# Neighbourhood attention with tokens in halves of the grid's columns: five transposes per pair of heads, and products with v over 128 and over 32 keys

## The chip, the cores and the metric

One core of one Trainium2 chip. The metric is the device time of one execution in microseconds; a smaller one is better. TensorE (PE in the rows, its weight loads PEld) multiplies and transposes, VectorE (DVE), ScalarE (ACT) and GpSimd (POOL) do the rest, and SyncE (SP) issues the transfers. Each has its own queue and works it off in order.

## The reference

Two layers, each with a gated feed-forward block, a mixer block and a second feed-forward block, with a layer norm behind every block. 256 tokens of 1024 numbers stand on a grid of 4 rows and 64 columns. The mixer projects x once and feeds three mixers: pooling over 2 to 16 neighbouring tokens, a short gated convolution, and neighbourhood attention. Its core:

```python
scores = jnp.einsum('brqhd,brikhd->bhrqik', q, kb).astype(jnp.float32) * (NA_HEAD_DIM ** -0.5)
scores = scores + bias.astype(jnp.float32)
scores = jnp.where(col_valid[:, None, :], scores, NEG_INF)
p = jax.nn.softmax(scores, axis=(-2, -1)).astype(v.dtype)
o = jnp.einsum('bhrqik,brikhd->brqhd', p, vb)
```

With 4 rows, every query sees all rows; in each it sees 16 of the 64 columns, chosen by its own column. There are 8 heads of 64 numbers. All is float32; the big products run as three products of float32r parts (upper by upper, upper by lower, lower by upper).

## The kernel before

**Tiling.** The tokens are two tiles of 128 (t), in the order of the sequence, so each tile has two grid rows. Each block streams its weights: SP loads 512 KB into one of 6 raw buffers (`raw`, L206), ACT casts it to float32r (`whi`, L218), DVE subtracts (`wlo`, L223), and TensorE multiplies (L345 to L347 with x stationary, L358 to L360 with the weights stationary, L370 to L372 for the projection back).

**Order of the work.** All engines take their instructions in the order in which the program is written. A `Pacer` keeps a clock of the work given to TensorE so far: `step(us)` moves it on, and hooks put in with `at(delay, tag, fn)` are written out at the first step behind their due time. So a delay such as A_TR sets after how many projection matmuls a piece stands on TensorE, and in what place on the others; it waits for nothing by itself. The waits come from the data and from the buffers.

**Attention.** The mixer projects v and the pooling input, then q0, k0, q1, k1 (four heads each), gc and h, and then the way back. For each half of the heads (q = 0, 1) there are two pairs of heads (j = 0, 1), and each pair goes through four hooks:

- `scores`: a block b of 128 queries is half of the columns (32) in all 4 rows. Each block and head (e) gets one product with 160 keys (4 rows of KW = 40 columns, L799), in a bank of the pool `acc`. DVE adds bias and mask (L808) and takes the maximum (L810); ACT takes the exponential (L813) into `pz`, a buffer of zeros that has all 64 columns per row.
- `normalise`: DVE multiplies by the inverse sum (L823, L825).
- `transposed`: `pz` has zeros outside of the 40 columns, so 256 keys are transposed per block and head: four transposes per head (L834) into one bank, and one copy by ACT (L839, `PT`).
- `weighted`: products of v with PT over 128 keys twice, 256 queries at once (L848), for both heads into one bank; ACT casts the result for each block (L861, `yT`) and DVE takes the lower part (L862).

The banks for projections, transposes and products come from one pool of four (`bank()`, tag mm); a fifth use waits until an earlier one has been read. The work tiles Sb and PT come from a pool of five. The bias of the second half is added by POOL (L690).

Of the kernel before, what the change touches and what calls it, by code (L numbers as in the profile page):

```python
# [16 lines left out]
P = 128  # L17
SEQ = 256
# [24 lines left out]
PZ = 4  # L43
# [14 lines left out]
A_TR = 2.2  # L58
A_PV = 1.4
# [85 lines left out]
def encoder_kernel(  # L145
# [14 lines left out]
    tp = ctx.enter_context(tc.tile_pool(name="tp", bufs=5))  # L160
    ap_ = ctx.enter_context(tc.tile_pool(name="ap", bufs=6))
# [18 lines left out]
    def mirrored(v):  # L180

        dims = [list(d) for d in v.ap]
        step, n = dims[-1]
        dims[-1] = [-step, n]
        return bass.AP(tensor=v.tensor, offset=v.offset + (n - 1) * step, ap=dims)

# [179 lines left out]
    def r_stat(ps, key, act, t, n, first, last, c=slice(0, 512), again=False):  # L366

        hi, lo = pc.get(key)
        ts = slice(t * P, (t + 1) * P)
        PE.matmul(ps, act[0][:, ts], hi[:, n, c], start=first, stop=False, skip_group_check=again)  # L370
        PE.matmul(ps, act[1][:, ts], hi[:, n, c], start=False, stop=False, skip_group_check=again)  # L371
        PE.matmul(ps, act[0][:, ts], lo[:, n, c], start=False, stop=last, skip_group_check=again)  # L372
# [13 lines left out]
    def ln_rest(t, stats, store):  # L386
# [9 lines left out]
        for c in hs:  # L396
            DVE.scalar_tensor_tensor(xt[:, c], xt[:, c], rs[:, 0:1], b[:, c], ALU.mult, ALU.add)
            if store:
                SP.dma_start(out[0, t * P : (t + 1) * P, c], xt[:, c])
# [68 lines left out]
    def ffn(key, xT, next_gb, stop, store=False):  # L468
# [69 lines left out]
        def act(k):  # L538
            f = k[-1]
            return [hts[f // 2][:, i, f % 2, :] for i in range(2)]  # L540
# [62 lines left out]
    def setup():  # L603
# [61 lines left out]

        pz = []
        for i in range(PZ):
            z = cp.tile([P, 2, ROWS, GRID], F32, tag=f"pz{i}", name=f"pz{i}")
            POOL.memset(z, 0.0)
            pz.append(z)  # L670
        consts.update(pz=pz, npz=0)
# [26 lines left out]
    def mixers(l, xT, next_gb, stop):  # L698
# [7 lines left out]
        v = hp.tile([P, NT, 512], F32, tag="h", name=nm("v"))  # L706
        U = ap_.tile([P, 2, SEQ + 2 * PADL], F32, tag="a", name=nm("U"))
# [5 lines left out]
        def pool_means():  # L713
# [15 lines left out]
            def product():  # L729
# [4 lines left out]
                for j in range(2):  # L734
                    c = 12 + l * 2 + j
                    ACT.activation(ya[:, j, :], ps[:, j, :], AF.Copy, scale=cw[:, c : c + 1])
# [6 lines left out]
        for t in range(NT):  # L743
# [3 lines left out]
            ACT.copy(v[:, t, :], pv)  # L747
            pc.step(6 * MM512)
# [5 lines left out]
            def spread(t=t, un=un):  # L754
# [3 lines left out]
                ACT.copy(U[:, :, PADL + t * P : PADL + (t + 1) * P], tr[:, 0:2, :])  # L758
# [12 lines left out]
        def conv_mixer(z):  # L771
# [6 lines left out]
            DVE.tensor_tensor(s, s, GB, ALU.mult)  # L778
            new_y(1)
            ACT.copy(ys[1][:, 0], s)  # L780
            DVE.tensor_tensor(ys[1][:, 1], s, f32(ys[1][:, 0]), ALU.subtract)

        def attention(j, qT, kT, q):

            st = {}
            new = [consts["pz"][(consts["npz"] + e) % PZ] for e in range(2)]
            consts["npz"] += 2
            tag = f"a{q}"

            def inner(z, b):  # L790
                return z[:, b, :, b * KOFF : b * KOFF + KW]

            def scores():
# [9 lines left out]
                st["sm"] = []  # L803
                for e in range(2):
# [7 lines left out]
                    for b in range(2):  # L812
                        ACT.activation(  # L813
                            inner(new[e], b), Sb[:, b, :].rearrange("p (i k) -> p i k", k=KW),
                            AF.Exp, bias=mx[:, b : b + 1], accum_out=sm[:, b : b + 1],
                        )
                    st["sm"].append(sm)
                pc.at(A_NORM, tag, normalise)

            def normalise():  # L820
                for e in range(2):
                    sm = st["sm"][e]
                    DVE.reciprocal(sm, sm)  # L823
                    for b in range(2):
                        DVE.tensor_scalar(inner(new[e], b), inner(new[e], b), sm[:, b : b + 1], None, ALU.mult)  # L825
                pc.at(A_TR, tag, transposed)

            def transposed():
                st["PT"] = []
                for e in range(2):  # L830
                    tr = bank().rearrange("p (a b) -> p a b", a=2)
                    for kc in range(2):
                        for b in range(2):
                            PE.transpose(  # L834
                                tr[:, kc, b * P : (b + 1) * P],
                                new[e][:, b, 2 * kc : 2 * kc + 2, :].rearrange("p r c -> p (r c)"), ident,
                            )
                    t_ = tp.tile([P, 2, SEQ], F32, tag="t", name=nm("PT"))
                    ACT.copy(t_, tr)  # L839
                    st["PT"].append(t_)  # L840
                pc.at(A_PV, tag, weighted)

            def weighted():
                po = bank()[:, 0:SEQ].rearrange("p (b r c) -> p b r c", b=2, r=ROWS)
                for kc in range(2):
                    for e in range(2):
                        c0 = (4 * q + 2 * j + e) * HD
                        PE.matmul(  # L848
                            po[e * 64 : e * 64 + 64], v[:, kc, c0 : c0 + HD], st["PT"][e][:, kc, :],
                            start=(kc == 0), stop=(kc == 1),  # L850
                        )
# [3 lines left out]
                for b in range(2):  # L855
                    src = mirrored(po[:, b])
                    dst = [
                        y[:, i, j, :].rearrange("p (r c) -> p r c", c=GRID)[:, :, b * QB : (b + 1) * QB]
                        for i in range(2)
                    ]  # L860
# [5 lines left out]
        def qk(q):  # L866
            pq = proj(f"q{q}")
            qT = hp.tile([P, 2, 2, P], F32, tag="qk", bufs=4, name=nm("qT"))
            for j in range(2):
                for b in range(2):  # L870
                    src = mirrored(pq[:, j, :].rearrange("p (r c) -> p r c", c=GRID)[:, :, b * QB : (b + 1) * QB])
# [87 lines left out]
```

## Time and profile before

| | us |
|---|---|
| median of 3 runs | 949.89 (949.8 to 949.92) |
| the profiled execution | 950.0 |
| its span, first to last instruction | 948.2 |
| TensorE busy | 938.1 (99%) |
| DVE, ACT, POOL busy | 577.5, 447.0, 60.9 |
| transposes L834, busy | 8.9 (64 of them) |
| products L848, busy | 7.8 (64 records of 32 products) |
| scores L799, busy | 5.4 (64 records of 32 products) |

A matmul of float32 operands shows as two records. Records overlap, because the array is pipelined: what a matmul costs is the distance from its start to the next one's start, not its duration. "x16" merges neighbours of one kind. The chain of work lists, in order of time, what ended last; a wait is put down to the engine and line that released it.

### The profile page before, as it was taken

Reading aid. Unit: us, or ns where it says so; the run is one execution under the profiler, and the core shown is the slowest. Engines: PE = TensorE matmul, PEld = TensorE weight load, DVE = VectorE, ACT = ScalarE, POOL = GpSimd, SP = SyncE. Lnnn points to the kernel's source line nnn. Section 1 sums busy time; section 2 is a strip of 40 time slices with the busy share of each in tenths; the row PEclk is TensorE's granted clock in tenths of the full one; section 3 lists DMA queues with packets and bytes.
Section 4 is the critical chain, followed back from the end, with each engine's and each line's share of the span. In section 5 each row is a group of like instructions: output and inputs, shape, how many; then the busy total and the mean of one; then the engine's idle time right before and its main releaser. Section 6 shows DMA issues by size and latency. Waiting matters only on the chain.

```text
span 948.2 us, 12782 instructions
## 1 busy us (share of the span) xinstructions
PE 938.1 (99%) x4819; PEld 793.6 (84%) x4819; DVE 577.5 (61%) x723; ACT 447.0 (47%) x622; POOL 60.9 (6%) x106
## 2 busy tenths in 40 slices
PE   9999999999999999999999999999999999999996
PEld 6888888989988888888888888888898888888895
DVE  5854454686777654555675555557777875554535
ACT  6644444346735544443444444444565554444420
POOL 4000100005100000000000001000060000000000
PEclk9999999999999999999999999999999999999999
DMA  9877486447444866655458657654645457656401
GB/s 324 304 256 226 107 297 194 133 139 239 153 137 156 270 233 185 196 182 163 144 172 264 233 157 224 212 173 143 201 151 174 156 188 249 217 189 194 161 1 45
DMA packets 96590, 178.81 MB, mean 189 GB/s; under 512 B 14784, under 2 KB 35856, under 8 KB 96528
## 3 DMA queue, kind: packets, MB, share of 16 engines
q1 hardware_dynamic: 96240, 177.60, 58.4%
q8 instruction: 38, 0.62, 0.3%
q10 hardware_dynamic: 288, 0.39, 0.1%
q14 instruction: 24, 0.20, 0.1%
HBM read 176.84 MB, written 1.13 MB: 188 GB/s over the span
## 4 chain that ended last, share of the span: by engine, by line
PE 99%; DVE 1%; ACT 0%; issue 0%; DVEq 0%
PE mm L347 17%; PE mm L345 17%; PE mm L346 17%; PE acc L370 10%; PE acc L371 10%; PE acc L372 10%; PE mm L358 4%; PE mm L360 4%; PE mm L359 4%; PE mm L477 2%; PE mm L323 1%; PE mm L834 1%; PE mm L848 1%; PE acc L799 1%; PE acc L309 0%; PE mm L757 0%
## 5 line engine op out<-in xcount | busy, mean ns | idle before, releaser
L223 DVE TENSOR_TENSOR wlo<-raw,whi 128x1024 fp32r<-128x1024 f32 (+1 forms) x322 | 389.8, 1234 | 209.8 <-ACT whi L218 209.5
L218 ACT CAST whi<-raw 128x1024 fp32r<-128x1024 f32 (+1 forms) x322 | 332.5, 1044 | 319.5 <-PE mm L346 150.6
L345 PE MATMUL mm<-whi,xhi 128*128 128x512 f32 x704 | 275.8, 392 | 0.3 <-ACT whi L218 0.3
L347 PE MATMUL mm<-wlo,xhi 128*128 128x512 f32 x704 | 274.4, 390 | 0.2 <-DVE wlo L223 0.2
L346 PE MATMUL mm<-whi,xlo 128*128 128x512 f32 x704 | 274.0, 389 | 0.0
L347 PEld LDWEIGHTS mm<-wlo,xhi 128*128 128x128 f32 x704 | 132.1, 188 | 28.8 <-DVE wlo L223 1.0
L345 PEld LDWEIGHTS mm<-whi,xhi 128*128 128x128 f32 x704 | 132.3, 188 | 28.4 <-ACT whi L218 1.1
L346 PEld LDWEIGHTS mm<-whi,xlo 128*128 128x128 f32 x704 | 132.3, 188 | 26.9
L370 PE MATMUL acc<-whi,hT 128*128 128x512 f32 (+1 forms) x352 | 138.4, 393 | 0.0
L371 PE MATMUL acc<-whi,hT 128*128 128x512 f32 (+1 forms) x352 | 136.5, 388 | 0.0
L372 PE MATMUL acc<-wlo,hT 128*128 128x512 f32 (+1 forms) x352 | 136.5, 388 | 0.0
L358 PE MATMUL mm<-xhi,whi 128*128 128x256 f32 x320 | 92.0, 287 | 0.0
L360 PE MATMUL mm<-xhi,wlo 128*128 128x256 f32 x320 | 90.5, 283 | 0.0
L359 PE MATMUL mm<-xlo,whi 128*128 128x256 f32 x320 | 90.5, 283 | 0.0
L372 PEld LDWEIGHTS acc<-wlo,hT 128*128 128x128 f32 x352 | 66.1, 188 | 13.6
L482 DVE TENSOR_TENSOR hT<-mm,hT 128x256 fp32r<-128x256 f32 x80 | 32.4, 423 | 73.1 <-ACT hT L481 73.1
L370 PEld LDWEIGHTS acc<-whi,hT 128*128 128x128 f32 x352 | 66.2, 188 | 12.7
L371 PEld LDWEIGHTS acc<-whi,hT 128*128 128x128 f32 x352 | 66.2, 188 | 12.6
L358 PEld LDWEIGHTS mm<-xhi,whi 128*128 128x128 f32 x320 | 61.3, 192 | 1.7 <-issue 1.5
L359 PEld LDWEIGHTS mm<-xlo,whi 128*128 128x128 f32 x320 | 61.3, 192 | 0.3
L360 PEld LDWEIGHTS mm<-xhi,wlo 128*128 128x128 f32 x320 | 61.3, 192 | 0.0
L393 POOL TENSOR_TENSOR rs<-rs,half_t 128x1 f32<-128x1 f32 x12 | 11.7, 979 | 637.5 <-DVE rs L392 637.5
(110 smaller groups left out, 584.2 us busy)
## 6 DMA issues: line engine op xcount, KB each, us to landing
raw<-in_ffn_w_up_dram SPq DMA_DIRECT2D x88, 512.0 KB, 4.6
raw<-in_ffn_w_down_dram SPq DMA_DIRECT2D x88, 512.0 KB, 4.4
raw<-in_ffn_w_gate_dram SPq DMA_DIRECT2D x87, 512.0 KB, 4.6
raw<-in_w_in_dram SPq DMA_DIRECT2D x40, 512.0 KB, 4.1
raw<-in_w_out_dram SPq DMA_DIRECT2D x16, 512.0 KB, 4.9
lng<-in_ln_g_dram SPq DMA_DIRECT2D x6, 512.0 KB, 5.4
lnb<-in_ln_b_dram SPq DMA_DIRECT2D x6, 512.0 KB, 6.5
rbias<-tab SPq DMA_DIRECT2D x16, 96.0 KB, 4.3
```

What stands on the lines that cost most here:

```text
L218: ACT.copy(u, r)
L223: DVE.tensor_tensor(d, r, f32(u), ALU.subtract)
L345: PE.matmul(ps, xT[0][:, kc, ts], hi[:, j, :], start=(kc == 0), stop=False)
L346: PE.matmul(ps, xT[1][:, kc, ts], hi[:, j, :], start=False, stop=False)
L347: PE.matmul(ps, xT[0][:, kc, ts], lo[:, j, :], start=False, stop=(kc == KC - 1))
L358: PE.matmul(o, hi[:, j, c], xT[0][:, kc, :], start=(kc == 0), stop=False)
L359: PE.matmul(o, hi[:, j, c], xT[1][:, kc, :], start=False, stop=False)
L360: PE.matmul(o, lo[:, j, c], xT[0][:, kc, :], start=False, stop=(kc == KC - 1))
L370: PE.matmul(ps, act[0][:, ts], hi[:, n, c], start=first, stop=False, skip_group_check=again)
L371: PE.matmul(ps, act[1][:, ts], hi[:, n, c], start=False, stop=False, skip_group_check=again)
L372: PE.matmul(ps, act[0][:, ts], lo[:, n, c], start=False, stop=last, skip_group_check=again)
L482: DVE.tensor_tensor(h[:, 1, :, ts], src, f32(h[:, 0, :, ts]), ALU.subtract)
```

## The change

A tile of tokens is now one half of the grid's columns in all 4 rows, instead of two whole rows. x is loaded and the result stored in that order (4 pieces of 32 tokens), and what needs the order of the sequence (pooling, convolution, k) is put back by access patterns. With that, v's tile b holds the 128 keys that lie in the columns of block b itself. A block sees 40 columns: 32 of its own, and 8 of the other half, that is 32 keys more. So the probabilities are written as `own` (128 per block and head) and `other` (32 per block and head); four transposes take own, and one takes other for both blocks and both heads at once. The products run over 128 keys (L878) and over 32 keys (L880), the latter in four groups of rows of the array. The 32 keys of v have to stand in the partitions of their group: v is stored to memory and read back in four pieces (`vr`). The exponential stays in place in Sb; the zeroed buffers are gone.

```diff
-PZ = 4
+PZ = 2
-A_TR = 2.2
-A_PV = 1.4
+A_TR = 3.2
+A_PV = 1.6
...
-        queue.dma_start(xs[t][:, c], x[0, t * P : (t + 1) * P, c])
+        src = x[0, :, c].rearrange("(r b q) d -> b r q d", b=NT, q=QB)[t]
+        queue.dma_start(xs[t][:, c], src)
...
+        vr = cp.tile([P, 512], F32, tag="vr", name=nm("vr"))
+        def other_keys():
+            at = tc.dram_tile([P, NT, 512], F32, name=f"v{l}")
+            SP.dma_start(at, v)
+            for b in range(2):
+                c0 = 0 if b == 0 else 2 * QB - KW
+                src = at[:, 1 - b].rearrange("(r c) d -> r c d", c=QB)[:, c0 : c0 + KW - QB]
+                for e in range(2):
+                    SP.dma_start(vr[(2 * b + e) * QB : (2 * b + e + 1) * QB, :], src)
...
             ACT.copy(v[:, t, :], pv)
+            if t == 1:
+                other_keys()
...
             def normalise():
+                own = pzp.tile([P, 2, 2, ROWS, QB], F32, tag="own", name=nm("pz"))
+                other = pzp.tile([P, 2, 2, ROWS, others], F32, tag="other", name=nm("pz"))
...
-                        DVE.tensor_scalar(inner(new[e], b), inner(new[e], b), sm[:, b : b + 1], None, ALU.mult)
+                        for dst, keys in zip((own, other), parts[b]):
+                            DVE.tensor_scalar(
+                                dst[:, b, e], st["S"][e][:, b, :, keys], sm[:, b : b + 1], None, ALU.mult
+                            )
...
             def transposed():
+                own, other = st["pz"]
+                tr = bank().rearrange("p (e b n) -> p e b n", e=2, b=2)
                 for e in range(2):
+                    for b in range(2):
+                        PE.transpose(tr[:, e, b, :], own[:, b, e].rearrange("p r k -> p (r k)"), ident)
+                main = tp.tile([P, 2, 2, P], F32, tag="t", name=nm("PT"))
+                ACT.copy(main, tr)
+                tr = bank()[:, 0:P]
+                PE.transpose(tr, other.rearrange("p b e r k -> p (b e r k)"), ident)
+                other = tp.tile([P, P], F32, tag="t", name=nm("PR"))
+                ACT.copy(other, tr)
...
             def weighted():
-                po = bank()[:, 0:SEQ].rearrange("p (b r c) -> p b r c", b=2, r=ROWS)
+                po = [bank()[:, 0:P] for _ in range(2)]
+                main, other = st["PT"]
+                for long in (True, False):
+                    for b in range(2):
+                        for e in range(2):
+                            c = slice((4 * q + 2 * j + e) * HD, (4 * q + 2 * j + e + 1) * HD)
+                            g = slice((2 * b + e) * QB, (2 * b + e + 1) * QB)
+                            o = po[b][e * 64 : e * 64 + 64]
+                            if long:
+                                PE.matmul(o, v[:, b, c], main[:, e, b, :], start=True, stop=False)
+                            else:
+                                PE.matmul(
+                                    o, vr[g, c], other[g, :], start=False, stop=True, tile_position=(g.start, e * 64)
+                                )
...
-            ACT.copy(kT, pk)
+            for j in range(2):
+                ACT.copy(in_tiles(kT[:, j, :]), tiled(pk[:, j, :]))
```

**Where the pieces stand on TensorE, first half of the heads.** Before, the transposes of both pairs of heads (pz0 to pz3, a bank per head) stand in the projection of k1 (mm_414):

```order
L834 MATMUL mm_416_2300<-ident_101,pz0_733 128x128 [waits DVE_49,PE_49,Pool_49]
L834 MATMUL mm_416_2300<-ident_101,pz0_733 128x128 [waits DVE_49]
L834 MATMUL mm_416_2300<-ident_101,pz0_733 128x128 x2
L834 MATMUL mm_418_2307<-ident_101,pz1_735 128x128 [waits DVE_49,PE_49,Pool_49]
L834 MATMUL mm_418_2307<-ident_101,pz1_735 128x128 [waits DVE_49]
L834 MATMUL mm_418_2307<-ident_101,pz1_735 128x128 x2
L834 MATMUL mm_420_2314<-ident_101,pz2_737 128x128 [waits PE_49,DVE_49,Activation_49,Pool_49]
L834 MATMUL mm_420_2314<-ident_101,pz2_737 128x128 [waits DVE_49]
```

Now they are ten, again in the projection of k1 (mm_419), twelve matmuls later:

```order
L857 MATMUL mm_421_2327<-ident_104,pz_412_2257 128x128 [waits DVE_49,PE_49]
L857 MATMUL mm_421_2327<-ident_104,pz_412_2257 128x128 [waits DVE_49] x3
L861 MATMUL mm_423_2334<-ident_104,pz_413_2258 128x128 [waits DVE_49,PE_49]
L857 MATMUL mm_425_2338<-ident_104,pz_414_2269 128x128 [waits DVE_49,PE_49,Activation_49]
L857 MATMUL mm_425_2338<-ident_104,pz_414_2269 128x128 [waits DVE_49] x3
L861 MATMUL mm_427_2345<-ident_104,pz_415_2270 128x128 [waits DVE_49,Activation_49]
```

The last one's wait for ACT is for the copy of mm_421, whose bank it takes.

**The products of the first half.** Before, they stand between two projections, each pair of heads with one bank:

```order
L848 MATMUL mm_428_2360<-PT_417_2305,v_325_1810 64x256 [waits Activation_49]
L848 MATMUL mm_428_2360<-PT_419_2312,v_325_1810 64x256
L848 MATMUL mm_428_2360<-PT_417_2305,v_325_1810 64x256
L848 MATMUL mm_428_2360<-PT_419_2312,v_325_1810 64x256
L848 MATMUL mm_430_2370<-PT_421_2319,v_325_1810 64x256 [waits Activation_49]
L848 MATMUL mm_430_2370<-PT_423_2326,v_325_1810 64x256 [waits Activation_49]
```

Now they stand inside the next projection (gc, mm_436), between the scores of the second half's first pair of heads (acc_437, acc_438) and those of its second pair. PT is the transposed `own`, PR the transposed `other`:

```order
L816 MATMUL acc_438_2390<-kT_431_2364,qT_411_2252 128x160
L878 MATMUL mm_445_2409<-PT_422_2332,v_325_1805 64x128 [waits PE_49]
L878 MATMUL mm_445_2409<-PT_422_2332,v_325_1805 64x128
L878 MATMUL mm_446_2410<-PT_422_2332,v_325_1805 64x128 x2
L880 MATMUL mm_445_2409<-PR_424_2336,vr_326_1806 64x128 [waits DMAHW6_49]
L880 MATMUL mm_445_2409<-PR_424_2336,vr_326_1806 64x128 [waits DMAHW7_49]
L880 MATMUL mm_446_2410<-PR_424_2336,vr_326_1806 64x128 [waits DMAHW0_49]
L880 MATMUL mm_446_2410<-PR_424_2336,vr_326_1806 64x128 [waits DMAHW1_49]
L878 MATMUL mm_448_2424<-PT_426_2343,v_325_1805 64x128 [waits PE_49,Activation_49]
L878 MATMUL mm_448_2424<-PT_426_2343,v_325_1805 64x128
L878 MATMUL mm_449_2425<-PT_426_2343,v_325_1805 64x128 [waits DVE_49]
L878 MATMUL mm_449_2425<-PT_426_2343,v_325_1805 64x128
```

The wait of mm_449 for DVE is for the subtraction that reads mm_445 (L891). In the second half of the heads the products stand inside the first matmuls of the way back, and the fourth output's wait for DVE there is for the reading of the projection h (L925).

**The same place on ACT.** Before, the four casts of the products (yT, L861) stand ahead of the exponentials of the second half (L813):

```order
L876 COPY kT_427_2358<-mm_414_2272 128x512 [waits PE_49]
L861 CAST yT_429_2365<-mm_428_2360 128x4x32 [waits PE_49]
L861 CAST yT_429_2365<-mm_428_2360 128x4x32 [waits DVE_49]
L861 CAST yT_429_2365<-mm_430_2370 128x4x32 [waits PE_49]
L861 CAST yT_429_2365<-mm_430_2370 128x4x32 [waits DVE_49]
L218 CAST whi_432_2382<-raw_383_2105 128x1024 [waits DMAHW4_49]
L813 ACTIVATE pz0_733,sm_439_2408<-Sb_437_2404,mx_438_2406 128x4x40 [waits DVE_49]
```

Now four exponentials stand ahead of them:

```order
L906 COPY kT_431_2364<-mm_419_2287 128x2x4x32
L228 CAST whi_434_2373<-raw_384_2107 128x1024 [waits DMAHW1_49]
L830 ACTIVATE Sb_439_2395,sm_441_2399<-Sb_439_2395,mx_440_2397 128x160 [waits DVE_49,Activation_49]
L830 ACTIVATE Sb_439_2395,sm_441_2399<-Sb_439_2395,mx_440_2397 128x160
L830 ACTIVATE Sb_442_2402,sm_444_2406<-Sb_442_2402,mx_443_2404 128x160 [waits DVE_49,PE_49,Activation_49]
L830 ACTIVATE Sb_442_2402,sm_444_2406<-Sb_442_2402,mx_443_2404 128x160
L890 CAST yT_447_2419<-mm_445_2409 128x128 [waits PE_49]
L890 CAST yT_447_2419<-mm_446_2410 128x128 [waits PE_49]
```

On SP, the store of v and the four readings of vr stand ahead of the last load of the projection weights (the second half of h). The second layer has the same order throughout.

More of the change, by code (lines that the diff above doesn't have):

```diff
@@ L368, in r_stat @@
         hi, lo = pc.get(key)
[L369 to L372, printed above, removed]
+        PE.matmul(ps, act[0][t], hi[:, n, c], start=first, stop=False, skip_group_check=again)
+        PE.matmul(ps, act[1][t], hi[:, n, c], start=False, stop=False, skip_group_check=again)
+        PE.matmul(ps, act[0][t], lo[:, n, c], start=False, stop=last, skip_group_check=again)
     gbs = []
@@ L539, in act @@
             f = k[-1]
-            return [hts[f // 2][:, i, f % 2, :] for i in range(2)]
+            return [[hts[f // 2][:, i, f % 2, t * P : (t + 1) * P] for t in range(NT)] for i in range(2)]
         def bias_ahead():
@@ L757, in spread @@
                     PE.transpose(tr[:, j, :], un[:, j * P : (j + 1) * P], ident)
-                ACT.copy(U[:, :, PADL + t * P : PADL + (t + 1) * P], tr[:, 0:2, :])
+                dst = U[:, :, PADL : PADL + SEQ].rearrange("p j (r b c) -> p j b r c", b=NT, c=QB)[:, :, t]
+                ACT.copy(dst, tr[:, 0:2, :].rearrange("p j (r c) -> p j r c", c=QB))
                 DVE.tensor_copy(GB[:, :, t * P : (t + 1) * P], tr[:, 2:4, :])
@@ L777, in conv_mixer @@
                     DVE.scalar_tensor_tensor(s[:, j, :], z[:, j, k : k + SEQ], tap[k], s[:, j, :], ALU.mult, ALU.add)
-            DVE.tensor_tensor(s, s, GB, ALU.mult)
+            yb = ap_.tile([P, 2, SEQ], F32, tag="a", name=nm("yb"))
+            for j in range(2):
+                DVE.tensor_tensor(tiled(yb[:, j, :]), in_tiles(s[:, j, :]), tiled(GB[:, j, :]), ALU.mult)
             new_y(1)
-            ACT.copy(ys[1][:, 0], s)
-            DVE.tensor_tensor(ys[1][:, 1], s, f32(ys[1][:, 0]), ALU.subtract)
+            ACT.copy(ys[1][:, 0], yb)
+            DVE.tensor_tensor(ys[1][:, 1], yb, f32(ys[1][:, 0]), ALU.subtract)
         def attention(j, qT, kT, q):
             st = {}
-            new = [consts["pz"][(consts["npz"] + e) % PZ] for e in range(2)]
-            consts["npz"] += 2
             tag = f"a{q}"
-            def inner(z, b):
-                return z[:, b, :, b * KOFF : b * KOFF + KW]
+            others = KW - QB
+            parts = [(slice(b * others, b * others + QB), slice((1 - b) * QB, (1 - b) * QB + others)) for b in range(2)]
             def scores():
@@ L830, in transposed @@
+                tr = bank().rearrange("p (e b n) -> p e b n", e=2, b=2)
                 for e in range(2):
[L831 to L837, printed above, removed]
@@ L852, in weighted @@
+                po = [p_.rearrange("p (r c) -> p r c", r=ROWS) for p_ in po]
                 if ys[2 + q] is None:
@@ L855, in weighted @@
                 for b in range(2):
[L856 to L860, printed above, removed]
+                    src = mirrored(po[b])
+                    dst = [tiled(y[:, i, j, :])[:, b] for i in range(2)]
                     ACT.copy(dst[0], src)
@@ L893, in mixers @@
         POOL.memset(z[:, :, SEQ + 1 :], 0.0)
-        DVE.tensor_tensor(z[:, :, 1 : SEQ + 1], p_, gc, ALU.mult)
+        for j in range(2):
+            DVE.tensor_tensor(in_tiles(z[:, j, 1 : SEQ + 1]), tiled(p_[:, j, :]), tiled(gc[:, j, :]), ALU.mult)
         conv_mixer(z)
```

40 lines of the change are left out of this document (16 added, 24 removed).

## The prediction

> **What bounds the kernel now.** I read the engines' busy shares first, then the chain of work that ended last, then TensorE's waits. The quoted rows are in that order.
>
> ```profile
> PE 938.1 (99%) x4819; PEld 793.6 (84%) x4819; DVE 577.5 (61%) x723; ACT 447.0 (47%) x622; POOL 60.9 (6%) x106
> ...
> PE 99%; DVE 1%; ACT 0%; issue 0%; DVEq 0%
> ...
> PE acc L309 <- DVE zeros L304: 1.5, 1, 1.5
> PE mm L345 <- ACT whi L218: 0.3, 1, 0.3
> PE mm L347 <- DVE wlo L223: 0.2, 1, 0.2
> ```
>
> TensorE is the chain, and it waits 2.0 us in all, at the start of the program. So time moves in two ways only: by what TensorE's own instructions take, and by any new wait on TensorE. Work on ACT, DVE or a queue counts only where TensorE comes to wait for it. The attention's pieces in the chain, in order of time (start, us, what), are these; of the second layer, its transposes:
>
> ```profile
> 240.47 2.36 PE mm L834 x16
> 245.69 1.88 PE mm L848 x16
> 249.19 1.29 PE acc L799 x16
> ...
> 258.71 1.77 PE mm L834 x16
> 263.35 1.88 PE mm L848 x16
> ...
> 706.46 2.37 PE mm L834 x16
> ...
> 724.72 1.77 PE mm L834 x16
> ```
>
> L834 are transposes, L848 the products with v, L799 the scores. One half of the heads (I call them q0 and q1) has 16 transposes, 16 product instructions and 16 score instructions. In q0 the transposes take 2.36 us, in q1 1.77 (0.11 each for 128 columns); q0's are longer because each new group waits for the normalising on DVE.
>
> **Price of a product and of a change of shape.** TensorE's rows around the products and the scores of q0 and q1 (start, us, operation):
>
> ```profile
> 245.29 0.28 PE L359 MATMUL mm<-xlo,whi 128*128 128x256 f32 x1
> 245.41 0.28 PE L360 MATMUL mm<-xhi,wlo 128*128 128x256 f32 x1
> 245.62 1.95 PE L848 MATMUL mm<-PT,v 128*64 128x256 f32 x16
> 247.50 0.39 PE L358 MATMUL mm<-xhi,whi 128*128 128x256 f32 x1
> 247.72 0.28 PE L359 MATMUL mm<-xlo,whi 128*128 128x256 f32 x1
> ...
> 246.32 0.39 PE L848 MATMUL mm<-PT,v 128*64 128x256 f32 x2
> 246.53 0.39 PE L848 MATMUL mm<-PT,v 128*64 128x256 f32 x2
> 246.75 0.39 PE L848 MATMUL mm<-PT,v 128*64 128x256 f32 x2
> ...
> 248.91 0.28 PE L360 MATMUL mm<-xhi,wlo 128*128 128x256 f32 x1
> 249.12 1.36 PE L799 MATMUL acc<-kT,qT 64*128 64x160 f32 x16
> 250.41 0.39 PE L358 MATMUL mm<-xhi,whi 128*128 128x256 f32 x1
> 250.63 0.28 PE L359 MATMUL mm<-xlo,whi 128*128 128x256 f32 x1
> ```
>
> Products already run two at a time (x2): a pair of 256 columns starts every 0.215 us. By columns that is 0.135 for a pair of 160 and 0.108 for 128, near the 0.11 of a 128-column transpose. A block of another tile shape pays at its edges. Into the products the step is 0.21 us (245.41 to 245.62) where 0.12 is usual: 0.09. The block lasts 1.88 us for eight pairs, 1.72: 0.16 more. Behind it the next step is 0.22 instead of 0.12: 0.10. Together 0.35 for two changes of shape. The scores give 0.09, 0.21 (1.29 less eight times 0.135) and 0.10, so 0.40. I take 0.18 per change.
>
> **Transposes.** Ten stand where sixteen stood, 1.10 us at 0.11. The tenth waits: the projection in progress holds one of the four banks, the first three results take the others, so the fourth result needs the first copied out. By the first two of these rows,
>
> ```profile
> L834 PE MATMUL mm<-ident,pz 128*128 128x128 f32 x64 | 8.9, 281 | 0.0
> ...
> L839 ACT COPY PT<-mm 128x512 f32<-128x512 f32 x16 | 8.8, 593 | 2.8 <-PE mm L834 2.4
> ...
> 240.46 0.52 DVE L825 TENSOR_SCALAR pz<-pz,sm 128x160 f32<-128x160 f32 x2
> ```
>
> the fourth transpose starts at 0.33 and takes 0.28, the copy 0.59, and some 0.1 goes to the two handovers (estimate), so the tenth starts at 1.31 and the block ends at 1.42. Against 2.36 and 1.77 that saves 0.94 in q0 and 0.35 in q1, **1.29 per layer**. Without the bank wait it would be 1.93; with q0's normalising still late, about 0.9. I take 1.29: the transposes now stand twelve matmuls later (1.4 us) behind a normalising of 16 shorter instructions instead of 8, which by the third row (0.52 for two of 160 columns) ends some 0.5 us later (estimate).
>
> **Products, apart from waits.** Per half: before, eight pairs of 0.215, 1.72 us. After, 128 columns over 128 keys: eight pairs of 0.108, 0.86; and 128 columns over 32 keys, 16 instructions in four groups of rows and two of columns. The trace shows two tiles side by side, in column groups (L848) and in row groups (L799); four at once it does not show. If four run at once, these are 0.43, if two, 0.86. So the columns save 0.43 or nothing. But shapes now change three times more per half (128 keys, 32, 128, 32 where one shape stood): 3 x 0.18 = 0.54. Net **+0.11** per half by four at once, +0.54 by two. I take four, since both kinds of grouping are seen at work. [...]
>
> **The new wait.** In q0, the changed program runs scores of the first pair of heads, both pairs' products, then scores of the second pair. Each pair's output now takes two banks. Of the four, the projection (mm_436) holds one, mm_445, mm_446 and mm_448 the rest; mm_449 must wait until mm_445 has been read by ACT (L890) and DVE (L891). On ACT that cast stands behind four exponentials of the scores just made. Their chain, from rows of q1 before, and the reading of a product from q0:
>
> ```profile
> 250.04 0.49 DVE L808 TENSOR_TENSOR Sb<-acc,bias 128x320 f32<-128x320 f32 x1
> 250.56 0.49 DVE L810 TENSOR_REDUCE mx<-Sb 128x2 f32<-128x320 f32 x1
> ...
> 251.09 0.43 ACT L813 ACTIVATE pz<-Sb,mx 128x160 f32<-128x160 f32 x1 [1.64 <-DVE mx L810]
> ...
> 252.43 0.41 ACT L813 ACTIVATE pz<-Sb,mx 128x160 f32<-128x160 f32 x1
> ...
> 252.92 0.43 ACT L813 ACTIVATE pz<-Sb,mx 128x160 f32<-128x160 f32 x1
> ...
> 246.75 0.27 ACT L861 CAST yT<-mm 128x128 fp32r<-128x128 f32 x1 [0.44 <-PE mm L848]
> ...
> 247.05 0.29 DVE L862 TENSOR_TENSOR yT<-mm,yT 128x128 fp32r<-128x128 f32 x1 [2.55 <-ACT yT L861]
> ```
>
> From the scores' start (249.12) to the first sum is 0.92; from there to ACT's first slot behind four exponentials 2.88 (252.92); from the cast to the subtraction 0.30, the subtraction 0.29, the handover 0.08 (estimate). So mm_449 may start **4.47 us** after the scores did. TensorE arrives there after four score pairs 0.54, three changes of shape 0.54, four pairs over 128 keys 0.43, the 32-key rounds 0.22, and mm_448's two pairs 0.22: **1.95**. It stands 2.5 us, and behind the waiting row the second scores and the rest of the projection stand too. Bounds: 2.3 with 32-key products two at a time, 3.1 with free changes of shape. In q1 the fourth bank is the projection that DVE reads at once (L925), so no such wait.
>
> **Costed at nothing.** The store of v and its four read-backs enter SP's queue ahead of the last projection load:
>
> ```profile
> 213.01 0.59 ACT L747 COPY v<-mm 128x512 f32<-128x512 f32 x1 [0.49 <-PE mm L347]
> ...
> 223.07 1.05 ACT L218 CAST whi<-raw 128x1024 fp32r<-128x1024 f32 x1 [2.38 <-PE mm L359]
> ...
> raw<-in_w_in_dram SPq DMA_DIRECT2D x40, 512.0 KB, 4.1
> ```
>
> v is ready at 213.6; a store of 512 KB by the last row takes 4.1, four issues 1.7, so that load goes out near 219.5 instead of 213.8 and lands at 223.6. Its cast, by its place in the program, is the one at 223.07: about half a microsecond late on ACT, while TensorE reads those weights after 257. Weight loads behind it are back in step by 223. vr itself lands near 222 and is read near 247. Without this cover, up to 6 us per layer. The strided x and output transfers keep their sizes; kT in two copies, the longer normalising and the shorter PT copies lie beside TensorE's projections.
>
> **Sum.** Per layer: -1.29 + 2 x 0.11 + 2.5 = +1.43; two layers +2.9. The profiled execution took 950.0 us around its span of 948.2, 0.1 above the median of 949.89. So 952.9 by it, **952.8 us** by the median: slower by 0.3%.
>
> **Rivals.**
> *No wait at mm_449* (faster). Place: that row. It decides if mm_445 is free within 1.95 us of the scores' start; then the rest counts alone, 2 x (-1.29 + 0.22): 947.7. For it: before, the cast followed the products by 0.1 (246.75 within the block), so ACT can be prompt. Against it: the four exponentials need these very scores. 6%.
> *The gains eat the wait* (no change). Shape changes between 128 and 32 rows are free and the tenth transpose waits for no bank: -1.93 - 2 x 0.43 + 3.1 = +0.3 per layer, 950.5. Against it: the edges of both blocks above. 12%.
> *Dearer pieces* (slower still). 32-key products go two at a time and each extra change costs 0.36: +1.08 per half; TensorE then arrives 0.75 later and waits 1.75: -1.29 + 2.16 + 1.75 = +2.6 per layer, 955.1. 10%.
> *The array slows after the pause.* The row of q0's products and q1's scores (TensorE, its weights, DVE, ACT, POOL, granted clock, DMA) has the clock at 1.00, without a pause to test it:
>
> ```profile
> 243.00:252.00 9.00, 9.00 (x80) 7.75 (x79) 5.63 (x12) 5.04 (x12) 0.00 (x0) 1.00 0.44 132
> ```
>
> If the clock fell to half for as long as the pause, +1.25 per layer more, 955.3. 5%. [...]
> *My forecast*: 67%.
>
> **How the numbers follow.** The forecast with its own bounds runs from 951.8 to 954.2 (waits of 2.3 to 2.7, halves of 0.0 to 0.5). To hold 8 in 10, I reach halfway to the no-change rival and to the two slower ones: 951.1 to 955.2. A measurement of this kernel tells about 0.2%, 1.9 us, from no change. Faster by more: 6%. Within: 13%, the no-change rival and a sliver of the forecast. Slower: 81%.
>
> **What would show it.** Right: a TensorE wait of 2.2 to 2.8 us per layer just ahead of the third group of 128-key products in q0, released by DVE's subtraction (L891), none in q1; transposes of about 1.4 us in both halves; q1's product block at 2.1 to 2.3 us. Wrong: no such idle, the wait at another row (vr's landing, the normalising), a 32-key block near 0.43 us per pair of heads, or SP's queue holding back weights that TensorE then waits for.

## The result, and the profile after

The changed kernel takes **974.17 us** (median of 5 runs, 972.06 to 975.51) against 949.89 (949.80 to 949.95): 24.3 us more, a ratio of 1.0251 with a 95% interval of 1.0239 to 1.0263. The forecast was 952.8, with a range of 951.1 to 955.2. The profiled execution took 974.46 us around a span of 972.7, against 948.2 before.

Busy time by engine, the chain of work that ended last, and TensorE's waits (us in total, times, longest) in the changed kernel:

```profile
PE 943.9 (97%) x4859; PEld 796.9 (82%) x4859; DVE 580.6 (60%) x759; ACT 443.9 (46%) x626; POOL 52.7 (5%) x102
...
PE 92%; DVE 3%; DMA 2%; issue 1%; ACT 1%; SPq 0%; DVEq 0%; ACTq 0%
...
PE acc L334 <- DMA x<-in_x_dram: 7.3, 3, 3.4
PE mm L878 <- DVE yT L891: 4.5, 2, 2.3
PE acc L320 <- DVE zeros L315: 1.5, 1, 1.5
PE mm L356 <- ACT whi L228: 0.9, 1, 0.9
```

The second wait is the one forecast, at its row, with its releaser: 2.3 us in each layer. The first was not forecast at all. It belongs to the start of the program, where x is transposed for the first time.

To find where 24.5 us of span went, I put the same projection and feed-forward matmuls of the two traces side by side and took the difference of their start times. It stays constant for hundreds of microseconds and steps in four places only. Here it is for all the kernels below (us; the tail is the rest of the difference of the spans). Each trace is of one execution, and that need not be the median one: the one of `after_rows_io` is the slowest of its four, those of the last three `rows2` kernels are the fastest of theirs.

```
                  span    start   layer 0  layer 1   tail
before            948.2
after             972.7  +10.4    +4.0     +5.3     +4.8
before_block_io   964.0  +10.1     0.0      0.0     +5.7
after_plain_io    956.6   -0.1    +4.4     +5.2     -1.2
after_rows_io     963.7   +5.2    +5.7     +5.1     -0.5
after_filled      972.3  +11.0    +4.3     +4.0     +4.8
rows2             960.2   +4.8    +4.9     +2.4     -0.1
rows2_fill10      956.1   +2.9    +2.7     +2.4     -0.1
rows2_pv          953.1   +5.3    -0.2     -0.1      0.0
rows2_pv_pool     950.7   +4.1    -0.9     -0.9     +0.2
repaired          949.4   +2.9    -0.9     -0.9     +0.1
repaired_wait     958.6   +2.9    +3.2     +4.4      0.0
repaired_fill     954.4   +2.9    +1.6     +1.6      0.0
best              947.1   +0.7    -0.9     -0.9     -0.1
```

So 15.2 us of the loss lie at the two ends of the program, outside the attention, and 9.3 in its two layers, where the forecast had 2.9.

**The start.** The share of the 16 DMA engines that is busy (tenths) and GB/s in the first 30 us, in 40 slices; the kernel before, then the change:

```profile
DMA  0039899999999999999997999999999889598998
GB/s 0 0 87 290 265 385 363 328 363 350 352 382 393 385 410 391 393 393 391 385 385 257 126 319 374 330 369 341 371 385 421 352 254 377 199 202 317 311 333 314
```

```profile
DMA  0009426999625899978998997999932222669999
GB/s 0 0 4 90 100 81 191 307 330 385 188 78 130 218 325 371 363 169 191 325 205 167 347 216 147 319 232 298 360 112 98 98 98 98 117 197 382 314 352 396
```

Look at the run of 98s, from 22.5 to 25.5 us: a quarter of the 392 or so that the kernel before reaches, with two tenths of the engines busy. Four of sixteen are working, and four is the number of blocks of 32 rows in the new source of an x load. The trace's completion events of single transfers say the same:

```
transfer                 before                      after
x, tile 0, columns 0:2   16, 2.86 to 3.45            1 at 2.10, then 4, 6.44 to 6.57
x, tile 1, columns 4:8   16, 8.26 to 10.18           1 at 6.77, then 4, 20.35 to 21.40
raw weights behind them  16, 9.67 to 11.51           12, 11.84 to 12.22, and 4, 21.79 to 22.48
```

The weights use all sixteen engines, and a quarter of each load stands in line behind x on the four. Of the 10.4 us at the start, 8.1 is more waiting on TensorE (10.1 against 2.0 in the first 40 us); the rest was not taken apart, but the granted clock was at 0.50 from 7.95 to 11.36 and from 21.62 to 25.01, where the kernel before has it at 1.00. The output's stores are confined in the same way: the first has one event at 956.21 and then 4, from 960.68 to 961.44; before, a store's 16 stand from 945.31 to 945.47. DMA share and rate in 40 slices from 963.0 to the span's end with the change, and from 943.4 to the end before:

```profile
DMA  1100024206001231222222222222222211100000
GB/s 68 51 17 0 0 51 43 9 0 26 0 9 60 60 68 60 85 102 94 102 102 102 102 102 102 102 102 102 102 102 102 102 77 60 43 9 0 0 0 0
```

```profile
DMA  0000000497998989899110000000000000000000
GB/s 0 0 0 0 0 0 0 171 461 307 444 358 341 427 341 427 341 341 342 51 68 0 0 17 0 0 0 0 0 0 0 0 0 0 0 0 0 0 0 0
```

The trace of the kernel before has the same pattern in two small loads. `rows<-in_pool_scale_dram`, with 4 rows outermost, has one event at 68.21 and then 4, from 69.02 to 69.06; `rows<-in_conv_w_dram`, with 12 rows, has one at 67.84 and then 12, from 68.63 to 68.87. What the early event is was not shown.

**The layers.** TensorE's rows of q0 in the first layer: transposes, first scores, products, and the projection behind them (start, us, operation):

```profile
252.22 0.62 PE L857 MATMUL mm<-ident,pz 128*128 128x128 f32 x4
252.76 0.30 PE L861 MATMUL mm<-ident,pz 128*128 128x128 f32 x1
253.15 0.58 PE L857 MATMUL mm<-ident,pz 128*128 128x128 f32 x2
253.94 0.67 PE L857 MATMUL mm<-ident,pz 128*128 128x128 f32 x2 [0.21 <-DVE pz L847]
254.52 0.30 PE L861 MATMUL mm<-ident,pz 128*128 128x128 f32 x1
254.58 0.36 PE L369 MATMUL mm<-xhi,whi 128*128 128x256 f32 x1
...
257.63 0.81 PE L816 MATMUL acc<-kT,qT 64*128 64x160 f32 x8
258.37 0.66 PE L878 MATMUL mm<-PT,v 128*64 128x128 f32 x8
258.96 0.45 PE L880 MATMUL mm<-PR,vr 32*64 32x128 f32 x8
259.33 0.44 PE L878 MATMUL mm<-PT,v 128*64 128x128 f32 x4
262.04 0.44 PE L878 MATMUL mm<-PT,v 128*64 128x128 f32 x4 [2.26 <-DVE yT L891]
262.41 0.45 PE L880 MATMUL mm<-PR,vr 32*64 32x128 f32 x8
...
264.20 0.41 PE L370 MATMUL mm<-xlo,whi 128*128 128x256 f32 x1
264.42 0.41 PE L371 MATMUL mm<-xhi,wlo 128*128 128x256 f32 x1
```

Three things are to be seen. The wait of 2.26 us stands before the third group of 128-key products. Behind it a projection matmul starts every 0.21 us where 0.12 was usual. And q0's transposes run from 252.22 to 254.58, 2.36 us, no shorter than the 2.28 between the same two starts before, because DVE normalises late:

```profile
240.30 2.52 PE L834 MATMUL mm<-ident,pz 128*128 128x128 f32 x16
242.58 0.36 PE L358 MATMUL mm<-xhi,whi 128*128 128x256 f32 x1
```

The granted clock (the third figure from the right) in the stretches with the pause and behind it, both layers:

```profile
257.50:263.00 5.50, 3.24 (x44) 2.02 (x44) 2.63 (x7) 2.69 (x12) 0.00 (x0) 1.00 0.76 270
263.00:268.00 5.00, 5.00 (x29) 4.53 (x28) 3.44 (x7) 2.42 (x11) 0.00 (x0) 0.66 0.06 5
727.50:733.00 5.50, 3.24 (x42) 1.99 (x40) 2.62 (x7) 2.58 (x11) 0.00 (x0) 0.87 0.72 270
733.00:739.00 6.00, 6.00 (x35) 5.15 (x28) 3.48 (x7) 2.29 (x10) 0.00 (x0) 0.55 0.03 2
```

### The profile page after: what moved, and what is told of

Read it like the earlier page. It is cut to its first block, busy times and chain, and to the rows that moved or that the text cites. A ratio compares the mean times of both kernels' runs of the same rounds, so it can differ in the third digit from the quotient of the medians.

```text
span 972.7 us, 12901 instructions
## 1 busy us (share of the span) xinstructions
PE 943.9 (97%) x4859; PEld 796.9 (82%) x4859; DVE 580.6 (60%) x759; ACT 443.9 (46%) x626; POOL 52.7 (5%) x102
## 4 chain that ended last, share of the span: by engine, by line
PE 92%; DVE 3%; DMA 2%; issue 1%; ACT 1%; SPq 0%; DVEq 0%; ACTq 0%
PE mm L356 16%; PE mm L358 16%; PE mm L357 16%; PE acc L380 10%; PE acc L381 10%; PE acc L382 10%; PE mm L369 3%; PE mm L371 3%; PE mm L370 3%; PE mm L487 2%; DMA x<-in_x_dram 2%; DVE wlo L233 1%; PE mm L334 1%; DVE pz L847 1%; DMA raw<-in_w_in_dram 1%
## 5 line engine op out<-in xcount | busy, mean ns | idle before, releaser
L491 ACT CAST hT<-mm 128x256 fp32r<-128x256 f32 x80 | 28.2, 374 | 43.8 <-PE mm L487 23.2
## 6 DMA issues: line engine op xcount, KB each, us to landing
raw<-in_ffn_w_up_dram SPq DMA_DIRECT2D x88, 512.0 KB
raw<-in_ffn_w_down_dram SPq DMA_DIRECT2D x88, 512.0 KB
raw<-in_ffn_w_gate_dram SPq DMA_DIRECT2D x87, 512.0 KB
raw<-in_w_in_dram SPq DMA_DIRECT2D x40, 512.0 KB
raw<-in_w_out_dram SPq DMA_DIRECT2D x16, 512.0 KB
lng<-in_ln_g_dram SPq DMA_DIRECT2D x6, 512.0 KB
lnb<-in_ln_b_dram SPq DMA_DIRECT2D x6, 512.0 KB
```

## The experiments

The theory after the two traces has four causes: x and output transfers on four engines (A); the wait at mm_449, as forecast; the array slowed by that pause (C); DVE late because SP's queue stood still. The rivals are named with each run. Of each edit only the telling lines are shown; ... stands for the others. Each kernel was timed beside the kernel before (949.86 to 949.95 in all groups).

**The transfers, undone and alone.** `after_plain_io` changes the load and the store back:

```diff
-        src = x[0, :, c].rearrange("(r b q) d -> b r q d", b=NT, q=QB)[t]
-        queue.dma_start(xs[t][:, c], src)
+        queue.dma_start(xs[t][:, c], x[0, t * P : (t + 1) * P, c])
...
-                SP.dma_start(out[0, :, c].rearrange("(r b q) d -> b r q d", b=NT, q=QB)[t], xt[:, c])
+                SP.dma_start(out[0, t * P : (t + 1) * P, c], xt[:, c])
```

> The changed kernel, only x loads and output stores as before (128 whole rows per transfer); tokens then stand in another order, so the output is another one, while every instruction on the engines stays. Theory A (an x transfer in four blocks of 32 rows is served by 4 of the 16 DMA engines, so the first loads and the last stores are late): the start gives back 10.4 us and the tail 4.9, so 959 us (958 to 961). Theory B (the late start is the changed setup or the queue's order, the tail something else): the time stays within 2 us of 974.

957.29 us (955.12 to 958.34), 1.0074 of before (1.0059 to 1.0089), 0.7 below the range. Theory A: start and tail are back, the layers keep their loss. The tail is even 1.2 shorter than before: the last stores landed that much sooner behind the same instructions.

`before_block_io` is the same edit the other way round, in the kernel before.

> The kernel before with only the x loads and output stores of the change; token order differs, so the output is another one, the instructions stay. Theory A: 949.9 + 10.4 + 4.9 = 965 us (963 to 967), each x load finished by 4 engines. Theory B: 950 to 952.

967.63 us (965.78 to 968.26), 1.0183 (1.0167 to 1.0198), 0.6 above the range. The two views alone, with no attention changed, cost 15.8 us of span in the fastest of the four, which is the one traced. That is most of the whole loss.

**Rows in one transfer.** `after_rows_io`:

```diff
-        queue.dma_start(xs[t][:, c], src)
+        for r in range(ROWS):
+            r0 = (r * NT + t) * QB
+            queue.dma_start(xs[t][r * QB : (r + 1) * QB, c], x[0, r0 : r0 + QB, c])
```

and likewise for the store, two rows of the grid by SP and two by ACT. The columns of x behind the first two blocks of 128 now come in one go per tile (four transfers), tile 1's issued by ACT.

> The changed kernel, each x load and output store as four transfers of 32 whole rows, half of them issued by ACT. Theory A, if 32 rows spread over all 16 engines: 959 us, plus up to 1.5 for the extra issues at the end (0.35 each). If such a transfer still reaches only 4 engines, or under theory B: 972 to 976.

961.54 us (960.53 to 965.47), 1.0129 (1.0107 to 1.0152), 1.0 above what theory A gave. Every piece now has 16 completion events, and the tail is back to within 0.5 us. The start is still 5.2 late: sixteen transfers instead of six, and SP takes from 3.61 to 9.32 for the issues of the last four, where an issue alone takes 0.3 to 0.4. The trace shows eight completion semaphores for all transfers of SP and ACT, and the held issues come 0.02 us behind the last event of the transfer that had the same semaphore before: SP's at 5.78 and 9.01 behind 5.76 and 8.99, ACT's at 6.44 behind 6.42. So here a ninth transfer in flight waited for one of the eight. The few engines were the first cause, and the many transfers are a second, read from the trace; no edit tried it alone.

**The pause filled.** `after_filled` adds, for the second pair of heads of q0:

```diff
+                for _ in range(FILL if (q, j) == (0, 1) else 0):
+                    for e in range(2):
+                        c = slice((4 * q + 2 * j + e) * HD, (4 * q + 2 * j + e + 1) * HD)
+                        PE.matmul(po[0][e * 64 : e * 64 + 64], v[:, 0, c], main[:, e, 0, :], start=True, stop=True)
```

> The changed kernel with 20 more pairs of products (128 keys, 64 columns each) into the first output bank of q0's second pair of heads, just ahead of the row that waits 2.3 us; the results are overwritten. They take 20 x 0.11 = 2.2 us, about the pause. Theory C (the pause itself lowers the clock granted behind it): projections behind it step at 0.12 instead of 0.21, 1.5 us less in the first layer and 2.8 in the second, so 970 us. Theory D (the clock falls for another reason, such as what the other engines do then): the slow steps stay, 974 to 975.

974.38 us (974.11 to 975.11), 1.0259 (1.0242 to 1.0277). The time did not move, and the trace says why: the 20 pairs stand in it as 80 records, two of each matmul, and took 4.4 us (259.93 to 264.35), and 1.7 of it came behind the release near 262.6. The slow steps are gone all the same. The same stretches as above:

```profile
258.00:264.90 6.90, 6.90 (x118) 6.08 (x116) 2.72 (x7) 2.67 (x11) 0.00 (x0) 1.00 0.62 218
264.90:270.00 5.10, 5.10 (x48) 4.65 (x47) 3.44 (x7) 3.19 (x13) 0.00 (x0) 1.00 0.00 0
728.00:735.00 7.00, 7.00 (x119) 6.18 (x121) 2.77 (x7) 2.71 (x11) 0.00 (x0) 1.00 0.60 214
735.00:741.00 6.00, 6.00 (x54) 5.55 (x55) 3.92 (x8) 4.14 (x14) 0.00 (x0) 1.00 0.10 15
```

**A base with 16 engines, and three edits on it.** `rows2` loads one row of the grid, both halves, per transfer, and stores by 32 rows:

```diff
+        src = x[0, r * GRID : (r + 1) * GRID, c].rearrange("(b q) d -> q b d", b=NT)
+        queue.dma_start(xall[r * QB : (r + 1) * QB, :, c], src)
...
```

> The changed kernel, x loaded by eight transfers (one row of the grid each, both halves of its columns; 32 blocks of 2 rows of x as the source's outer size) and stored by 32 whole rows; 128 x 256 columns first, then 768. Theory A (the transfer's outer size of 4 is what confines it to 4 engines; with 32 it reaches all 16): 10 us less at the start and 5 at the end, 958 to 960 us, and each x load finishes on 16 engines. Rival (the eight transfers in flight are the limit, as in the run with 32-row loads): 961 to 964.

961.77 us (959.90 to 964.04), 1.0126 (1.0110 to 1.0143): the rival's range, though each x load has its 16 events. The tail is back; the start is 4.8 late, with 2.9 of waiting for x. Note its second layer, +2.4 us: the pause is there, and this time no slow step followed (clock 1.00 from 728 to 733, against 0.66 behind the pause of the first layer). The pause does not always slow the array. Its first layer has one more wait on TensorE, 1.5 us of q0's scores for ACT's copy of kT.

`rows2_fill10` has the fill with 10 pairs.

> The kernel of the run above with 10 more pairs of products in the pause of q0. A pair took 0.22 us in the run with 20 of them (4.4 in all), so 10 fill the pause of 2.3 and no more. Theory C (the pause lowers the clock): the slow steps behind it vanish and nothing is added, 1.5 us less in the first layer and 2.5 in the second: 4 us less than the run above. Theory D: no less.

958.86 us (958.03 to 961.29), 1.0099 (1.0084 to 1.0114), 2.9 less than `rows2` where 4 were expected. Of the profile's 4.1, 1.9 came from the start, 2.2 from the first layer (0.7 of it a shorter wait for kT), none from the second, which had no slow steps to lose.

`rows2_pv` moves one due time of the order by 0.3:

```diff
-A_PV = 1.6
+A_PV = 1.3
```

> The kernel of the first run of this group with the products one step of 12 projection matmuls earlier (A_PV 1.3 for 1.6), so that they stand ahead of the scores and the cast of mm_445's successor stands ahead of the exponentials. If the wait is the casts behind the exponentials, it goes (2.3 per layer), and by theory C the slow steps too: 8 to 9 us less than the first run, 950 to 951. If only the wait goes: 4.6 less. If another wait takes its place (the probabilities' copies, the bank of the k projection): less than 3.

955.98 us (954.97 to 957.08), 1.0068 (1.0051 to 1.0085), 5.8 less than `rows2`. No wait for the subtraction is left in its trace, nor another in its place; by the table the two layers give back 5.1 and 2.5 us. Of the 5.1, 1.5 is the wait for kT, which is gone here though the edit did not aim at it. The expected 8 counts slow steps in both layers; the traced `rows2` had them in the first only, and of its other executions no trace tells.

`rows2_pv_pool` issues v's store and the read-backs from POOL:

```diff
-            SP.dma_start(at, v)
+            POOL.dma_start(at, v)
...
-                    SP.dma_start(vr[(2 * b + e) * QB : (2 * b + e + 1) * QB, :], src)
+                    POOL.dma_start(vr[(2 * b + e) * QB : (2 * b + e + 1) * QB, :], src)
```

> The run above with the store of v and its four read-backs issued by POOL instead of SP, so that SP no longer stands 6 us and the last projection loads go out 8 us earlier. If that delay made DVE late for q0's transposes (0.8 us per layer): 1.6 less than the run above. If TensorE never waited for it: the same within 0.5.

954.54 us (952.50 to 954.93), 1.0045 (1.0030 to 1.0060), 1.4 less; 0.7 and 0.8 us in the layers by the table (the traced start is 1.1 shorter too). SP's queue in the changed kernel shows what was in the way:

```profile
223.99 0.34 SPq L715 DMA_DIRECT2D v<-v  x1
229.82 2.66 SPq L720 DMA_DIRECT2D vr<-v  x4
232.61 0.38 SPq L216 DMA_DIRECT2D raw<-in_w_in_dram  x1
```

and DVE behind it, where three subtractions of weights now come together just ahead of the scores:

```profile
239.32 4.51 DVE L233 TENSOR_TENSOR wlo<-raw,whi 128x1024 fp32r<-128x1024 f32 x3 [5.95 <-PE mm L371]
243.76 0.48 DVE L825 TENSOR_TENSOR Sb<-acc,bias 128x320 f32<-128x320 f32 x1
...
249.64 0.15 DVE L844 RECIPROCAL sm<-sm 128x2 f32<-128x2 f32 x1
```

Normalising starts at 249.64; without the 10.37 that the start is late, that is 239.27, against 238.47 before: 0.8 late. With POOL's queue it starts at 242.60, without 4.14 of the start 238.46. The two rows, before and with POOL's queue:

```profile
238.47 0.15 DVE L823 RECIPROCAL sm<-sm 128x2 f32<-128x2 f32 x1
242.60 0.15 DVE L845 RECIPROCAL sm<-sm 128x2 f32<-128x2 f32 x1
```

**All repaired, and the forecast's own terms.** `repaired` loads x at first in whole rows, writes the transposes to the permuted columns in two copies each, loads x a second time in the new layout near 120 us, and keeps the last two edits:

```diff
+            for b in range(NT):
+                src = tr.rearrange("p n (r b c) -> p n b r c", b=NT, c=QB)[:, :, b]
+                to = slice(b * P + t * GRID, b * P + (t + 1) * GRID)
+                hi, lo = [v[:, ks, to].rearrange("p n (r c) -> p n r c", c=QB) for v in xT]
...
+            pc.at(100, "xr", reload_x)
```

> The change with every loss found so far taken out: x loaded first in 128 whole rows (its transposes copied to the permuted columns in two pieces), loaded again in the new layout around 100 us, output stored by 32 rows from SP and ACT, products ahead of the scores (A_PV 1.3), v's store and read-backs issued by POOL. If nothing else is lost, each layer keeps 1.0 us (transposes 1.3 less, products 0.2 more, as the last run's rows show): 949.9 - 2.0 = 948 us, 947.5 to 949, below the kernel before. If the extra copies or the second load delay TensorE, or the clock still falls: 950 to 953.

951.31 us (951.24 to 953.14), 1.0017 (1.0008 to 1.0026), the range given for extra copies that delay TensorE. The layers keep 0.9 each, near the 1.0 worked out; the start loses 2.9, behind ACT's extra copies (TensorE waits 2.6 us there for casts of weights).

`repaired_wait` has A_PV = 1.6 again.

> The run above with the products back where the change has them (A_PV 1.6), so only the wait at mm_449 is left of the losses. Theory C: 2.3 us of wait per layer and slow steps of 1.5 to 2.5 behind it, so 8 more than the run above: 956 to 957. If the wait alone counts: 952.6.

960.83 us (960.69 to 962.64), 1.0120 (1.0106 to 1.0135): 9.5 us for two waits and what follows them, where 8 was expected (the 956 to 957 counted from the 948 expected of `repaired`).

`repaired_fill` adds the 10 pairs to it.

> The run above with 10 more pairs of products in the pause. The wait stays as long, TensorE is busy in it. Theory C: only the 4.6 us of the two waits are left, 952 to 953. Theory D: no less than the run above.

956.38 us (956.27 to 958.23), 1.0074 (1.0059 to 1.0088). 4.45 us less than `repaired_wait`: the slowing. 5.07 more than `repaired`: two waits of 2.5 each. The expected 952 to 953 left out the start. With the array's pace kept, a layer costs +1.6 us against the kernel before, where the forecast had +1.43.

`best` lets the first transposes write the permuted columns themselves, so the copies are whole again:

```diff
+            if tag == "acc":
+                to = to.rearrange("p (b r c) -> p r b c", b=NT, c=QB)
+            PE.transpose(to, xs[t][:, (k0 + j) * P : (k0 + j + 1) * P], ident)
...
```

> The repaired kernel with its start mended: the first transposes of x write the permuted columns themselves (a strided result in the bank), so that ACT and DVE copy each in one piece again instead of two. The rows of the repaired run have TensorE 3.1 us late by 14 us, behind ACT's casts (2.6 us of waits), and 1.2 and 0.9 us gained in the two layers. If the extra copies cost the 3.1: 949.9 - 2.1 = 947.8 us (947.2 to 948.5), below the kernel before. If the strided result costs TensorE as much, or the second load of x or the output's 32-row stores hold the rest: 949.5 to 951.5.

948.88 us (948.73 to 949.17) against 949.95 (949.79 to 950.35), 0.9988 (0.9979 to 0.9997): 1.1 us faster, the only version here below the kernel before; the interval ends just under 1. The gain is smaller than the 2.1 expected: 0.7 us stay at the start, and the layers give 0.9 each, not 1.2 and 0.9. Its waits on TensorE:

```profile
PE acc L325 <- DVE zeros L320: 1.5, 1, 1.5
PE mm L370 <- ACT whi L228: 0.3, 1, 0.3
PE mm L370 <- ACT xhi L347: 0.3, 1, 0.3
```

## Why the prediction was wrong, point by point

The direction was right and the size was not. The step that failed most is a clause under "Costed at nothing": "The strided x and output transfers keep their sizes". True, and beside the point. The bytes stayed, the number of engines fell from 16 to 4. It cost 10.4 us at the start and 4.8 at the end, and could have been bounded from the profile: x and the first weights are used within the first 13 us with the engines at nine tenths, and at the end nothing hides a store. At 98 GB/s instead of 392, x's 1 MB takes four times as long. I gave these transfers no price; the one price of a transfer in my working, the row "512.0 KB, 4.1", is of a load on 16 engines.

*What bounds the kernel.* Right: everything lost was lost as TensorE's own time or as waits on it, save the tail.

*The wait at mm_449.* Right in place, releaser and size: 2.26 us idle forecast as 2.5, in q0 only, in both layers; mm_449 starts 4.41 us after the scores (257.63 to 262.04), forecast 4.47.

*The array slows after the pause.* Held for 5%, as a rival of +1.25 per layer; the 5% was my estimate, and the row it had beside it (243 to 252 us, clock 1.00) has no pause in it. It came, and was larger: 1.5 and 2.8 in `repaired_wait` over `repaired_fill`, with the clock at 0.72 and 0.56 behind the pause. It is not sure to come (the second layer of `rows2`), and this is the likely source of the changed kernel's spread of 3.5 us. A pause of 2.26 us was enough. In the traces of the kernel before and of the changed kernel the granted clock changes only at whole multiples of 3.413 us, counted from its first entry (at 6.12 and at 4.54 us): after 275 of them before; after 1, 2, 5, 6, 76, 77, 213, 215 and 281 with the change. The slow stretch of `rows2` is one such step long (0.66 over 5 us is 3.4 us at half). How much of the pause falls into one such step went with what followed. The steps around the pauses of the changed kernel, then around that of the second layer of `rows2` (second figure: TensorE busy):

```profile
260.55:263.94 3.39, 1.90 (x23) 1.39 (x24) 1.24 (x5) 1.70 (x9) 0.00 (x0) 1.00 0.45 170
263.96:267.36 3.40, 3.40 (x16) 3.13 (x14) 2.66 (x5) 1.86 (x8) 0.00 (x0) 0.50 0.00 0
728.18:731.57 3.39, 1.59 (x24) 0.83 (x22) 1.86 (x4) 1.94 (x10) 0.00 (x0) 1.00 0.93 348
731.59:738.40 6.81, 6.37 (x35) 5.20 (x36) 3.97 (x9) 2.51 (x12) 0.00 (x0) 0.50 0.01 5
```

```profile
722.81:726.21 3.40, 2.27 (x30) 1.39 (x28) 2.14 (x5) 1.65 (x6) 0.00 (x0) 1.00 1.01 367
726.23:729.62 3.39, 2.27 (x26) 1.76 (x27) 1.58 (x6) 1.33 (x8) 0.00 (x0) 1.00 0.18 69
729.64:733.03 3.39, 3.39 (x28) 3.28 (x27) 2.33 (x4) 2.95 (x11) 0.00 (x0) 1.00 0.02 5
```

In `rows2` an edge between two steps split the pause in halves, 1.13 us idle on either side, and the clock stayed. The other nine pauses in the five traces that have them left 1.5 to 2.3 us idle in one step, and one or two steps at half the clock followed. The wait of 1.50 us for kT in `rows2`, whole within one step, left the clock at 1.00, so a limit, if there is one, lies near 1.5; no run moved a pause to find it.

*The transposes.* q1: 0.33 saved in each layer (1.69 to 1.36 by the starts), forecast 0.35. q0: forecast to save 0.94, lost 0.08 in the first layer of the changed kernel and saved 0.26 in the second, because the normalising ended at 254.3 and not before the block. With v's transfers on POOL's queue the block took 1.67 us (245.88 to 247.55 in `rows2_pv_pool`), a saving of 0.61: the normalising, from 242.60 to 247.3, takes 1.0 us longer than before (238.47 to 242.2), where I had estimated 0.5.

*SP's queue.* I had named the cover rightly (TensorE reads the last weights late) and missed who else stands behind the late cast: DVE, whose subtractions for these weights push the scores and so the normalising back by 0.8 us. The load went out at 232.61, 8.4 us later than before once the start is taken off, not 5.7, since the store took 5.8 us and the read-backs' issues 2.7. ACT stands behind that load as well, and its copy of kT behind ACT's late casts: q0's scores wait for it on TensorE, 0.3 us in the changed kernel, 1.0 in `after_plain_io` and 1.5 in `rows2`, each in one layer, and not at all with POOL's queue. So "kT in two copies" did not always lie beside TensorE's projections.

*The products.* Four tiles of 32 x 64 did run at once: eight instructions of L880 start 7 ns apart in fours, and a 32-key block takes 0.38 us. q1's whole block runs 1.93 us from its start to the next matmul's (279.04 to 280.97), against 1.88 before, so +0.05 per half where +0.11 was forecast; with both edges it takes 2.11, forecast 2.1 to 2.3. The 0.18 for a change between 128 and 32 rows was my estimate, carried over from changes to and from the full array; each added 0.09 to the step into it (0.20 where 0.11 is usual).

*The sum.* Forecast 2.9: measured, with transfers and pace taken out and SP's queue free, 3.2 (`repaired_fill`, two layers). Per layer -0.61 - 0.33 + 2 x 0.05 + 2.5 = +1.66 by the terms, so the mechanism in the layers was right and the transposes' saving too large. Two figures of my range do not come out of their own words: waits of 2.3 to 2.7 and halves of 0.0 to 0.5 give 951.9 to 954.7, not 951.8 to 954.2, and half way from 954.2 to the slower rivals is 954.7, not 955.2. Neither comes near 974. To the 3.2 came 15.2 of transfers, some 4.3 of slow steps, and 1.6 of SP's queue: 24.3 of the 24.5.

The rival "no wait at mm_449" gave 947.7; `best`, which is that case with the start nearly mended, has 948.88.

## What to carry to other kernels

When a layout changes, count for every transfer not only its bytes but its outermost dimension on both sides, and read from the trace on how many engines such a transfer ends: here 4 blocks, at the source of the loads and at the destination of the stores, ended on 4 engines, and 128 rows on 16. At the two ends of this program nothing hid it (10.4 and 4.8 us). A wait on TensorE is not priced by its length alone (9.5 us for two of 2.26, with what followed, in `repaired_wait`): ask what pace the array has behind it, and if the order can be moved by one step, move it. A step "costed at nothing" on a queue needs the list of all who stand behind its landing, down to the engine that is not the bottleneck.

## What the runs showed that was not expected

An x load in four blocks of 32 rows ended on 4 engines, loads with 32 or 128 outer blocks on 16, and the four engines moved 98 to 102 GB/s together. Behind a pause of 2.26 us TensorE went on at one of two paces: as before it, or half, for 3.41 us in the first layer and 6.83 in the second, one and two steps of the granted clock; a pause split in halves by such a step's edge was followed by the first. A matmul of 32-bit floats appears twice in the trace, so 20 pairs of 128 columns took 4.4 us and not 2.2. At the start of `after_rows_io` no more than eight transfers of SP and ACT were in flight: the held ones were issued 0.02 us behind the end of the one that had their completion semaphore. A strided result of a transpose cost the array nothing: 0.60 us for four at the start in `best`, as in the kernel before.
